# Row sums of the first norm taken from x's column tiles by ScalarE and GpSimd, and the first seven-product block in the order m1 m2 m7 m6 m4 m5 m3 with PSUM banks of its own for m3

## The chip, the cores and the metric

The kernel runs on one NeuronCore of a Trainium2 chip. Its time is device microseconds of one execution, and the median of several executions is compared. The engines are named as in the profile: PE (TensorE, matmul), PEld (its weight loads), DVE (VectorE), ACT (ScalarE), POOL (GpSimd) and SP (SyncE, which here only issues DMAs). DMAs are issued on the queues of SP, ACT and POOL. Each engine takes its own instructions in the order in which the program lists them; engines wait for each other through semaphores.

## The reference

One layer of an encoder on 512 tokens of width 2048, batch 1, in float32:

```python
def rmsnorm(x, g):
    xf = x.astype(jnp.float32)
    y = xf * lax.rsqrt(jnp.mean(xf * xf, axis=-1, keepdims=True) + EPS)
    return (y * g.astype(jnp.float32)).astype(x.dtype)

h = rmsnorm(x, g_mix)
proj = jnp.einsum('bsd,de->bse', h, w_in)          # (512, 2048) @ (2048, 4608)
qa, ka, va, qb, kb, vb = jnp.split(proj, offs, axis=-1)
...
x = x + jnp.einsum('bse,ed->bsd', mixed, w_out)
h2 = rmsnorm(x, g_ffn)
gate, up = jnp.split(jnp.einsum('bsd,df->bsf', h2, w_gate_up), 2, axis=-1)
x = x + jnp.einsum('bsf,fd->bsd', jax.nn.silu(gate) * up, w_down)
return rmsnorm(x, g_final)
```

Between them stand two attention mixers. Only the first norm and the first part of the input projection matter here. The norm's row factor r1 (one number for each of the 512 tokens) does not enter the projection's operands: the projection is computed from x times g_mix, and r1 is multiplied in when a result leaves PSUM. So r1 is needed only from the first eviction that uses it.

## The kernel before

**Numbers.** Every float32 operand of a matmul is split in two parts (`split`): the high part is an ACT copy to the type float32r, the low part a DVE subtraction of source and high part. A product is three matmuls (`mm3`, lines 230 to 232: high by high, high by low, low by high), each of 128x128 weights on 512 columns.

**Units.** The work of PE is a list of units in a fixed order. For each unit n the main loop at the end of the function first prepares (`x_prep` of tile n+1 while n is below 16; `prepare`, which issues weight loads and weight splits for units up to a set number of microseconds ahead by the plan's own clock), then multiplies, then runs the hooks that other code has registered for n with `hook(n, f)`. So the order on every engine's queue is written out by this loop. At most 8 pairs of split weights (`tw`) exist, so splits are at most 8 units ahead.

**The first chunk, units 0 to 15.** It multiplies x with the 512 columns of w_in that give kA and vA. x arrives as 16 column tiles `xs[k]` (512 tokens by 128 columns, as 128x512), loaded by SP. `x_prep(k)` transposes the tile on PE into a PSUM bank, copies it on ACT with the gain into `xpair` (line 326), makes the high part on ACT (line 327) and the low part on DVE (line 328). The unit then runs 12 matmuls. Two and three units after each pair of tiles, `x_sums` (four DVE operations of 256 columns, line 348) and `x_split` (two ACT copies, line 343, and two DVE subtractions, line 344) make the sums of x's quarters that the seven-product blocks need. Before that, POOL copies one of the parts that they overwrite to DRAM (`ar`, line 331); the split waits for this copy. After unit 15 ACT evicts four banks to tiles and sends them to DRAM (`kvA`, line 464).

**The column blocks, units 16 to 71 and 72 to 127.** Each multiplies x with 1024 columns of w_in by a seven-product scheme (Strassen's in Winograd's form): seven products m1 to m7 of half the size in each direction, each 8 units of 6 matmuls, 336 matmuls a block. For m7, m6, m5 and m4 DVE first adds or subtracts two weight tiles (line 792), then splits (ACT line 755, DVE line 758); for m1, m2 and m3 there is only the split. The products are summed up in three pairs of PSUM banks: m1, m6, m5 and m3 on pair z, m7 and m4 on pair y, m2 on pair x. A result is made in two steps: `begin` copies a pair of banks to an `ends` tile on ACT (line 840), `close` adds another pair to it on DVE (line 845) and POOL stores it; `only` is a `begin` with a store by ACT. Each multiplies r1 in. Where a product goes on summing on banks that are still to be read, its first matmul waits for that eviction. The first block's order is m1 m2 m7 m6 m5 m4 m3, and m1 is evicted seven units after its end, because r1 is late; the second block's order is m1 m7 m6 m2 m5 m4 m3.

**Row sums.** For r1 the kernel reads x a second time: eight loads of 128 tokens by 1024 columns on SP's queue (line 360, 512 KB each, two buffers), and eight squares on ACT with a row sum as side result (line 363), hooked to units 13 to 28. `make_r1` at unit 29 adds the halves on DVE and raises to the power -1/2 on POOL (line 212).

**Homes.** Tiles of x and of weights land in `homes`, a first-in first-out list of 20 tiles of 128x512 (`stage`). `x_prep` gives x's tile back as soon as its transposes are listed; a weight tile comes back after its last use. From unit 21 `more_homes` adds four tiles, and `fewer_homes` takes them out again in the second block. A load into a home waits for the last reader of what was there.

Of the kernel before, what the change touches and what calls it, by code (L numbers as in the profile page):

```python
# [11 lines left out]
F32 = mybir.dt.float32  # L12
# [7 lines left out]
P = 128  # L20
S = 512
D = 2048
# [34 lines left out]
HEAD_RATE = (1.42, 1.9)  # L57
TURN_LAG = 6
VALUE_LAG = 8
COLUMN_BLOCKS = 2  # L60


# [5 lines left out]
def encoder_block(ctx, tc, x, g_mix, w_in, g_q_a, g_k_a, g_out_a, g_out_b, w_out, g_ffn,  # L68
# [15 lines left out]
    def slot(base, dtype=F32, shape=(P, 512)):  # L84
        return sp.tile(list(shape), dtype, tag="s", name=nm(base))
# [14 lines left out]
    def release(*tiles):  # L100
        banks.extend(tiles)
# [12 lines left out]
    extra_homes, retired = [], []  # L114

    def more_homes():
        more = wp.tile([P, 4, 512], F32, tag="more", bufs=1, name="more")
        extra_homes.extend(more[:, n] for n in range(4))
        homes.extend(extra_homes)

    def fewer_homes():
        kept = [h for h in homes if not any(h is e for e in extra_homes)]
        homes.clear()
        homes.extend(kept)
        retired.extend(extra_homes)

    def leave_homes():
        homing[0] = False
# [32 lines left out]
    nc.scalar.activation(slot("table")[:, :1], ones, AF.Copy)  # L161
    warm_ps = bank()

    def warm_up(n):
# [143 lines left out]
    def x_prep(k):  # L308
        ps = bank()
        for t in range(NT):  # L310
            nc.tensor.transpose(ps[:, t * P:(t + 1) * P], xs[k][:, t, :], ident)
        homes.append(xs[k].rearrange("p t c -> p (t c)"))
        i, half = divmod(k, 2)
        if half == 0:
            xpair[i] = in_turn(pairs_turn, 3, [P, 4 * 512], F32, "xpair")
        flat = xpair[i][:, half * 1024:half * 1024 + 512]
        view = flat.rearrange("p (f c) -> p f c", c=256)
        hi, lo = (arena[half][:, 0:2, i, j] for j in range(2))
        gain = gm[:, k:k + 1]
        if k == 0:  # L320
            ps3 = ps.rearrange("p (f c) -> p f c", c=256)
            nc.scalar.activation(hi, ps3, AF.Copy, scale=gain)
            nc.vector.scalar_tensor_tensor(lo, ps3, gain, f32(hi), op0=OP.mult, op1=OP.subtract)
            nc.scalar.activation(flat, ps, AF.Copy, scale=gain)
        else:
            nc.scalar.activation(flat, ps, AF.Copy, scale=gain)
            nc.scalar.activation(hi, view, AF.Copy)
            nc.vector.tensor_tensor(lo, view, f32(hi), op=OP.subtract)
        release(ps)
        if half == 0:  # L330
            hook(k, lambda: nc.gpsimd.dma_start(ar_dram[:, i], arena[0][:, 1, i]))
        else:
            hook(k + 2, lambda: x_sums(i))
            hook(k + 3, lambda: x_split(i))
# [16 lines left out]
        tt(s2, s1, a_l)  # L351
        tt(s4, b_l, s2)

    ss1 = small(2 * NT)
    rows, rows_turn = {}, []

    def load_rows(n):
        rows[n] = in_turn(rows_turn, 2, [P, D // 2], F32, "rows")
        t, half = divmod(n, 2)
        nc.sync.dma_start(rows[n], x[0, t * P:(t + 1) * P, half * (D // 2):(half + 1) * (D // 2)])  # L360

    def row_squares(n):
        nc.scalar.activation(rows[n], rows[n], AF.Square, accum_out=ss1[:, n:n + 1])

    for n, at in enumerate((13, 15, 18, 20, 22, 24, 26, 28)):
        hook(at - 3, lambda n=n: load_rows(n))
        hook(at, lambda n=n: row_squares(n))

    def col_sums(src):
        ps = bank()  # L370
# [8 lines left out]

    def make_r1():  # L380
        ss = small()
        nc.vector.tensor_reduce(ss, ss1.rearrange("p (t c) -> p t c", c=2), axis=AX.X, op=OP.add)
        r1["r"] = rsqrt_mean(ss, NT, D)
        r1["rs"] = small()
        nc.vector.tensor_scalar(r1["rs"], r1["r"], HD ** -0.5, None, op0=OP.mult)

    tabs = {}

    hook(29, make_r1)
    hook(21, more_homes)  # L390

    def table_tasks():
        tasks = []
# [367 lines left out]
            self.box.multiply(self)  # L761

    class ColBlock:
        def __init__(self, w, row, lo, pairs, plan, tag, ready=None, close=None, chain=CHAIN):
            self.pairs, self.plan, self.ready, self.close = pairs, plan, ready, close
            self.ps, self.at, self.held = {}, {}, []

            def raw(i, j, q):
                at = row + (2 * q + i) * P
                return Raw(lambda t: [(w[0, at:at + P, lo[j]:lo[j] + 512], t)], tag=tag, width=512)  # L770
            kinds = {"a": (0, 0), "b": (0, 1), "c": (1, 1), "d": (1, 0), "e": (0, 1), "f": (1, 0), "g": (1, 1)}
            self.raws = [{n: raw(i, j, q) for n, (i, j) in kinds.items()} for q in range(pairs)]
            order = [(form, q) for form in chain for q in range(pairs)]
            if ready is not None:
                rest = order[6:8] + order[8:3 * pairs] + order[3 * pairs + 6:]
                order = order[:6] + order[3 * pairs:3 * pairs + 6] + rest
# [16 lines left out]
            return t[dst]  # L793

        def bank_of(self, form):
            name = CHAIN_BANK[form]
            if name not in self.ps:
                self.ps[name] = [bank() for _ in range(2)]
            return self.ps[name]

        def multiply(self, u):
            dst, i = self.bank_of(u.form), u.i
            if self.ready is not None:
                drain_until(lambda: self.ready[i])
            ending = self.close is not None and u.form == "m3"
            if ending:
                self.held.append(u)
            for t in range(1 if ending else 2):
                mm3(dst[t], cols(form_of(u.form, i), t * P), (u.pair[:, 0], u.pair[:, 1]),
                    u.form in ("m1", "m7", "m2") and i == 0, i == self.pairs - 1, True)  # L810
            if ending and i == self.pairs - 1:
                self.close(self)

        def done(self, form):
            release(*self.ps.pop(CHAIN_BANK[form]))

        def after(self, form, late, f):
            hook(self.at[form] + late, f)
# [3 lines left out]
    def in_block(names, lo):  # L822
        first = not blocks
        box = ColBlock(w_in, 0, lo, KD // 2, REREAD, "craw0" if first else "craw",
                       chain=("m1", "m2", "m7", "m6", "m5", "m4", "m3") if first else CHAIN)
        blocks.append(box)
        out = {}

        def rows_of(form, i, j, f, late=0):
            box.after(form, late, lambda: [f(form, j, 2 * i + t, t) for t in range(2)])  # L830
            if form in LAST_OF_BANK:
                box.after(form, late, lambda: box.done(form))

        def begin(form, j, row, t):
            if not ends:
                ends.extend(sp.tile([P, 2, 512], F32, tag="ends", bufs=3, name=nm("ends")) for _ in range(3))
            if t == 0:
                ends.append(ends.pop(0))
            out[j, row] = ends[-1][:, t]
            nc.scalar.activation(out[j, row], box.bank_of(form)[t], AF.Copy,  # L840
                                 scale=row_scale_of(names[j])[:, row:row + 1])

        def close(form, j, row, t):
            e = out[j, row]
            nc.vector.scalar_tensor_tensor(e, box.bank_of(form)[t], row_scale_of(names[j])[:, row:row + 1], e,
                                           op0=OP.mult, op1=OP.add)
# [12 lines left out]

    blocks, ends = [], []  # L860

# [16 lines left out]
    last.after("m5", 0, fewer_homes)  # L878
# [481 lines left out]
```

## Time and profile before

| | before |
|---|---|
| three runs | 2024.49 us median, 2023.68 to 2028.52 |
| span of the profiled execution | 2023.3 us |
| mean granted TensorE clock | 0.996 |
| first matmul of unit 0 / of the first block / of the second block / behind it | 7.14 / 57.95 / 143.35 / 219.51 us |
| DMA | 394.81 MB, mean 195 GB/s |

Of the profiled execution only the span, from its first to its last instruction, is given; the runs' times contain what lies around it. In the profile's rows, times are microseconds from the span's start and durations are microseconds unless marked ns. A row of the timeline reads: start, duration, engine, line of the code, operation, output<-input by the program's names, shapes, count; in brackets the idle time of that engine before it and what ended it. A grouped row reads: line, engine, operation, names and shapes, count | busy us, mean ns of one | idle us before them, and what ended it. A row of busy times by stretch reads: start:end and length, then for each engine its busy time and number of instructions, the granted clock, the share of the 16 DMA engines' time, and GB/s. Matmuls are pipelined: one of 128x512 shows 0.39 us, but in an unbroken row they start 0.227 us apart.

### The profile page before, as it was taken

The numbers are of one execution on the slowest core, as the hardware profiler recorded it, in microseconds if no ns is written. First come the engines' busy times: TensorE is split into PE (matmuls) and PEld (weight loads), VectorE is DVE, ScalarE is ACT, GpSimd is POOL, SyncE is SP. The second block draws the span as 40 slices with busy tenths as digits, with TensorE's granted clock in tenths as the row PEclk, the third lists the DMA queues.
The fourth block names the chain that finished last, engine by engine and source line by source line (L and its number), as shares of the span: only waits on it lengthen the run. The fifth ranks groups of instructions, "written<-read, shape, count | busy, mean of one in ns | idle before, by whom it ended". The sixth has DMA issues, their size and how long they took to land. (4 is left out here: it accounts for less than half of the span.)

```text
span 2023.3 us, 27380 instructions
## 1 busy us (share of the span) xinstructions
PE 1989.5 (98%) x9019; PEld 1632.9 (81%) x9019; DVE 1558.8 (77%) x2771; ACT 1112.5 (55%) x1964; POOL 125.9 (6%) x155
## 2 busy tenths in 40 slices
PE   9999999999999999999999999999999999999997
PEld 7778887887788888888888888888888887788886
DVE  6778866576754688878877878778789887977977
ACT  6655344455553565555555555545546665666656
POOL 0000100000010000000000000000000121111122
PEclk9999999999999999999999999999999999999999
DMA  9777533335343546647647558458467698768855
GB/s 293 239 251 235 185 115 103 99 111 171 98 151 133 184 167 203 239 136 266 220 163 273 186 184 285 153 192 296 133 227 267 189 248 260 196 168 270 198 128 190
DMA packets 232671, 394.81 MB, mean 195 GB/s; under 512 B 21536, under 2 KB 70480, under 8 KB 232400
## 3 DMA queue, kind: packets, MB, share of 16 engines
q1 hardware_dynamic: 206032, 330.33, 48.5%
q0 software_dynamic: 14800, 32.51, 7.9%
q10 hardware_dynamic: 11696, 30.23, 4.3%
q8 instruction: 70, 1.15, 0.2%
q14 instruction: 73, 0.60, 0.1%
HBM read 329.28 MB, written 63.70 MB: 194 GB/s over the span
## 5 line engine op out<-in xcount | busy, mean ns | idle before, releaser
L230 PE MATMUL b<-tw,arena 128*128 128x512 f32 x2136 | 838.5, 393 | 7.2 <-ACT ends L840 2.5
L231 PE MATMUL b<-tw,arena 128*128 128x512 f32 x2136 | 834.0, 390 | 5.4 <-DVE tw L758 5.1
L232 PE MATMUL b<-tw,arena 128*128 128x512 f32 x2136 | 832.8, 390 | 0.0
L755 ACT ACTIVATE tw<-raw 128x512 fp32r<-128x512 f32 x924 | 559.3, 628 | 441.2 <-DVE raw L792 286.6
L758 DVE TENSOR_TENSOR tw<-raw,tw 128x512 fp32r<-128x512 f32 x924 | 619.3, 687 | 173.1 <-ACT tw L755 170.1
L231 PEld LDWEIGHTS b<-tw,arena 128*128 128x128 f32 x2136 | 401.6, 188 | 93.3 <-DVE tw L758 12.3
L230 PEld LDWEIGHTS b<-tw,arena 128*128 128x128 f32 x2136 | 401.4, 188 | 90.7 <-ACT tw L755 3.3
L232 PEld LDWEIGHTS b<-tw,arena 128*128 128x128 f32 x2136 | 401.4, 188 | 83.9
L792 DVE TENSOR_TENSOR raw<-raw,raw 128x512 f32<-128x512 f32 x528 | 361.7, 685 | 0.8 <-DMA raw<-in_w_gate_up_dram 0.6
L230 PE MATMUL b<-w,arena 128*128 128x512 f32 x368 | 146.7, 399 | 0.0
L232 PE MATMUL b<-w,arena 128*128 128x512 f32 x368 | 144.3, 392 | 0.0
L231 PE MATMUL b<-w,arena 128*128 128x512 f32 x368 | 144.1, 392 | 0.0
L1127 POOL DMA_DIRECT2D x1d<-ev x76 | 66.4, 977 | 1157.5 <-ACT ev L1126 1156.5
L232 PEld LDWEIGHTS b<-w,arena 128*128 128x128 f32 x368 | 69.5, 189 | 15.1
L231 PEld LDWEIGHTS b<-w,arena 128*128 128x128 f32 x368 | 69.6, 189 | 13.9
L230 PEld LDWEIGHTS b<-w,arena 128*128 128x128 f32 x368 | 69.5, 189 | 13.7
L758 DVE TENSOR_TENSOR tw<-stage,tw 128x512 fp32r<-128x512 f32 x93 | 62.2, 687 | 23.5 <-ACT tw L755 23.4
L755 ACT ACTIVATE tw<-stage 128x512 fp32r<-128x512 f32 x93 | 56.5, 627 | 41.8 <-DVE stage L792 29.5
L222 DVE TENSOR_TENSOR pTl<-b,pTh 128x512 fp32r<-128x512 f32 x64 | 44.0, 688 | 36.1 <-ACT pTh L221 25.4
L287 DVE TENSOR_TENSOR w<-raw,w 128x512 fp32r<-128x512 f32 x96 | 64.7, 684 | 5.7 <-ACT ends L840 3.0
L348 DVE TENSOR_TENSOR pair<-pair 128x256 f32<-128x256 f32 x120 | 45.5, 421 | 27.3 <-ACT pair L983 21.9
L1126 ACT ACTIVATE ev<-b,smalls 128x512 f32<-128x512 f32 x76 | 49.7, 683 | 29.2 <-PE b L232 28.0
(186 smaller groups left out, 1749.2 us busy)
## 6 DMA issues: line engine op xcount, KB each, us to landing
raw<-in_w_gate_up_dram SPq DMA_DIRECT2D x616, 256.0 KB, 5.3
raw<-in_w_down_dram SPq DMA_DIRECT2D x176, 256.0 KB, 6.9
stage<-in_w_in_dram SPq DMA_DIRECT2D x114, 256.0 KB, 5.1
forms<-pair SPq DMA_DIRECT2D x22, 896.0 KB, 5.3
x1d<-ev POOLq DMA_DIRECT2D x76, 256.0 KB, 6.6
fr<-forms ACTq DMA_DIRECT2D x35, 512.0 KB, 5.5
raw<-in_w_in_dram SPq DMA_DIRECT2D x64, 256.0 KB, 4.2
raw<-in_w_out_dram SPq DMA_DIRECT2D x32, 512.0 KB, 4.8
```

The costliest lines, as they stand in the source:

```text
L222: nc.vector.tensor_tensor(lo, src, f32(hi), op=OP.subtract)
L230: nc.tensor.matmul(dst, ah, bh, start=start, stop=False, skip_group_check=chained)
L231: nc.tensor.matmul(dst, ah, bl, start=False, stop=False, skip_group_check=chained)
L232: nc.tensor.matmul(dst, al, bh, start=False, stop=stop, skip_group_check=chained)
L287: nc.vector.tensor_tensor(self.w[1], self.src, f32(self.w[0]), op=OP.subtract)
L348: nc.vector.tensor_tensor(out, x, y, op=op)
L755: nc.scalar.activation(self.pair[:, 0], self.src, AF.Copy)
L758: nc.vector.tensor_tensor(self.pair[:, 1], self.src, f32(self.pair[:, 0]), op=OP.subtract)
L792: nc.vector.tensor_tensor(t[dst], t[src[0]], t[src[1]], op=OP.add if form == "m6" else OP.subtract)
L1126: nc.scalar.activation(e, box.bank_of(form)[t], AF.Copy, scale=r2["r"][:, row:row + 1])
L1127: nc.gpsimd.dma_start(x1_dram[2 * cb + j, row], e, accum_op=OP.add)
```

## The change

**Row sums.** The second reading of x goes. `row_squares(k)` is now called at the end of `x_prep(k)`: ACT squares the tile `xs[k]` in place after its transposes, and POOL adds the squares of tiles 1 to 15 to that of tile 0 in an accumulator `sq1` of 128x512. `make_r1` moves from unit 29 to unit 20 and reduces `sq1` over 128 columns for each of the four token groups. The tile goes back to `homes` after the square and the add, no longer after the transposes. The space of the two row buffers becomes four tiles `early`: one is the accumulator, three are additional homes until unit 12 (a tile of x that lies in one of them by then comes back to the list later).

**The first block.** m4 comes before m5. m3 sums up alone on two banks of its own (pair x, after m2's have been released), instead of on z. So m5, the last on z, is read twice: by the `close` of result (1,1), and by a `begin` of result (0,1), to which a `close` after m3 adds m3's banks. m1 is evicted right at its end. The second block is left as it was.

**Small.** The first ACT instruction, which loads the table, writes to a column of `smalls` instead of to a tile of its own. On PE's queue the number and kind of instructions are the same.

```diff
-    def more_homes():
-        more = wp.tile([P, 4, 512], F32, tag="more", bufs=1, name="more")
...
+    def more_homes(name, tile):
+        extra_homes[name] = [tile[:, n] for n in range(4)]
+        homes.extend(extra_homes[name])
...
 (x_prep)
             nc.tensor.transpose(ps[:, t * P:(t + 1) * P], xs[k][:, t, :], ident)
-        homes.append(xs[k].rearrange("p t c -> p (t c)"))
...
         release(ps)
+        row_squares(k)
...
-    def load_rows(n):
-        rows[n] = in_turn(rows_turn, 2, [P, D // 2], F32, "rows")
-        t, half = divmod(n, 2)
-        nc.sync.dma_start(rows[n], x[0, t * P:(t + 1) * P, half * (D // 2):(half + 1) * (D // 2)])
-
-    def row_squares(n):
-        nc.scalar.activation(rows[n], rows[n], AF.Square, accum_out=ss1[:, n:n + 1])
-
-    for n, at in enumerate((13, 15, 18, 20, 22, 24, 26, 28)):
-        hook(at - 3, lambda n=n: load_rows(n))
-        hook(at, lambda n=n: row_squares(n))
+    early = sp.tile([P, 4, 512], F32, tag="rowss", bufs=1, name="early")
+    more_homes("early", early)
+    sq1 = [homes.pop()]
+
+    def row_squares(k):
+        home = xs[k].rearrange("p t c -> p (t c)")
+        if k == 0:
+            nc.scalar.activation(sq1[0], home, AF.Square)
+        else:
+            nc.scalar.activation(home, home, AF.Square)
+            nc.gpsimd.tensor_tensor(sq1[0], sq1[0], home, op=OP.add)
+        homes.append(home)
...
-        nc.vector.tensor_reduce(ss, ss1.rearrange("p (t c) -> p t c", c=2), axis=AX.X, op=OP.add)
+        nc.vector.tensor_reduce(ss, sq1[0].rearrange("p (t c) -> p t c", t=NT), axis=AX.X, op=OP.add)
...
-    hook(29, make_r1)
-    hook(21, more_homes)
+    hook(20, make_r1)
+    hook(21, lambda: more_homes("more", wp.tile([P, 4, 512], F32, tag="more", bufs=1, name="more")))
+    hook(EARLY_HOMES, lambda: fewer_homes("early"))
...
 (ColBlock.__init__)
+            self.banks = dict(CHAIN_BANK, m3="x") if apart else CHAIN_BANK
+            self.last_of_bank = LAST_OF_BANK + ("m5",) if apart else LAST_OF_BANK
+            self.opening = ("m1", "m7", "m2") + (("m3",) if apart else ())
...
 (in_block)
-                       chain=("m1", "m2", "m7", "m6", "m5", "m4", "m3") if first else CHAIN)
+                       chain=("m1", "m2", "m7", "m6", "m4", "m5", "m3") if first else CHAIN, apart=first)
...
-        rows_of("m1", 0, 0, begin, 7 if first else 0)
+        rows_of("m1", 0, 0, begin)
...
-        rows_of("m5", 1, 1, close)
+        rows_of("m5", 1, 1, close, not first)
         rows_of("m4", 1, 0, close)
-        rows_of("m3", 0, 1, only)
+        if first:
+            rows_of("m5", 0, 1, begin)
+            rows_of("m3", 0, 1, close)
+        else:
+            rows_of("m3", 0, 1, only)
```

More of the change, by code (lines that the diff above doesn't have):

```diff
@@ L59 @@
 VALUE_LAG = 8
+EARLY_HOMES = 12
 COLUMN_BLOCKS = 2
@@ L113, in encoder_block, with fewer_homes @@
     homing = [True]
-    extra_homes, retired = [], []
-    def more_homes():
-        more = wp.tile([P, 4, 512], F32, tag="more", bufs=1, name="more")
[L118 to L122, printed above, removed]
+    extra_homes, retired = {}, []
+    def more_homes(name, tile):
+        extra_homes[name] = [tile[:, n] for n in range(4)]
+        homes.extend(extra_homes[name])
+    def fewer_homes(name):
+        kept = [h for h in homes if not any(h is e for e in extra_homes[name])]
         homes.clear()
         homes.extend(kept)
-        retired.extend(extra_homes)
+        retired.extend(extra_homes[name])
     def leave_homes():
@@ L160, in encoder_block @@
     nc.vector.memset(warm, 0.0)
-    nc.scalar.activation(slot("table")[:, :1], ones, AF.Copy)
+    nc.scalar.activation(small(1), ones, AF.Copy)
     warm_ps = bank()
@@ L352, in form_sums @@
         tt(s4, b_l, s2)
-    ss1 = small(2 * NT)
-    rows, rows_turn = {}, []
-    def load_rows(n):
-        rows[n] = in_turn(rows_turn, 2, [P, D // 2], F32, "rows")
-        t, half = divmod(n, 2)
-        nc.sync.dma_start(rows[n], x[0, t * P:(t + 1) * P, half * (D // 2):(half + 1) * (D // 2)])
-    def row_squares(n):
-        nc.scalar.activation(rows[n], rows[n], AF.Square, accum_out=ss1[:, n:n + 1])
-    for n, at in enumerate((13, 15, 18, 20, 22, 24, 26, 28)):
-        hook(at - 3, lambda n=n: load_rows(n))
-        hook(at, lambda n=n: row_squares(n))
+    early = sp.tile([P, 4, 512], F32, tag="rowss", bufs=1, name="early")
[9 more added lines that the diff above has]
+        homes.append(home)
     def col_sums(src):
@@ L763, in encoder_block, with __init__ @@
     class ColBlock:
-        def __init__(self, w, row, lo, pairs, plan, tag, ready=None, close=None, chain=CHAIN):
+        def __init__(self, w, row, lo, pairs, plan, tag, ready=None, close=None, chain=CHAIN, apart=False):
             self.pairs, self.plan, self.ready, self.close = pairs, plan, ready, close
+            self.banks = dict(CHAIN_BANK, m3="x") if apart else CHAIN_BANK
+            self.last_of_bank = LAST_OF_BANK + ("m5",) if apart else LAST_OF_BANK
+            self.opening = ("m1", "m7", "m2") + (("m3",) if apart else ())
             self.ps, self.at, self.held = {}, {}, []
@@ L795, in bank_of @@
         def bank_of(self, form):
-            name = CHAIN_BANK[form]
+            name = self.banks[form]
             if name not in self.ps:
@@ L809, in multiply @@
                 mm3(dst[t], cols(form_of(u.form, i), t * P), (u.pair[:, 0], u.pair[:, 1]),
-                    u.form in ("m1", "m7", "m2") and i == 0, i == self.pairs - 1, True)
+                    u.form in self.opening and i == 0, i == self.pairs - 1, True)
             if ending and i == self.pairs - 1:
@@ L814, in done @@
         def done(self, form):
-            release(*self.ps.pop(CHAIN_BANK[form]))
+            release(*self.ps.pop(self.banks[form]))
         def after(self, form, late, f):
@@ L824, in in_block, with rows_of @@
         box = ColBlock(w_in, 0, lo, KD // 2, REREAD, "craw0" if first else "craw",
-                       chain=("m1", "m2", "m7", "m6", "m5", "m4", "m3") if first else CHAIN)
+                       chain=("m1", "m2", "m7", "m6", "m4", "m5", "m3") if first else CHAIN, apart=first)
         blocks.append(box)
         out = {}
[L829 to L832, printed above, removed]
+        def rows_of(form, i, j, f, ending=True):
+            box.after(form, 0, lambda: [f(form, j, 2 * i + t, t) for t in range(2)])
+            if form in box.last_of_bank and ending:
+                box.after(form, 0, lambda: box.done(form))
         def begin(form, j, row, t):
@@ L877, in encoder_block @@
     last.after("m3", 0, leave_homes)
-    last.after("m5", 0, fewer_homes)
+    last.after("m5", 0, lambda: fewer_homes("more"))
     last.after("m3", 1, lambda: reload("qA0", qA[0]))
```

## The prediction

> **What bounds the kernel now.** I read the page first, then the busy time of three stretches, then the waits of PE inside the one that the change touches.
>
> ```profile
> span 2023.3 us, 27380 instructions
> PE 1989.5 (98%) x9019; PEld 1632.9 (81%) x9019; DVE 1558.8 (77%) x2771; ACT 1112.5 (55%) x1964; POOL 125.9 (6%) x155
> ```
>
> PE is the bound over the whole span, so a change off PE pays only where PE stands still. From the timeline of PE, the first chunk's 16 units run from 7.14 to 57.95 us, the first column block from 57.95 to 143.35, the second from there to 219.52. The busy time of these stretches:
>
> ```profile
> core 0: us, PE busy (x) PEld busy (x) DVE busy (x) ACT busy (x) POOL busy (x), PEclk, DMA share, GB/s
> 7.14:57.95 50.81, 50.81 (x254) 41.87 (x253) 37.28 (x71) 38.59 (x68) 4.45 (x8) 1.00 0.91 288
> ...
> 57.95:143.35 85.40, 80.01 (x337) 63.50 (x336) 64.93 (x111) 48.88 (x85) 4.37 (x7) 0.98 0.74 261
> 143.35:219.52 76.17, 76.17 (x338) 63.07 (x337) 59.59 (x102) 38.29 (x64) 3.79 (x7) 1.00 0.70 230
> ```
>
> Both column blocks have 336 matmuls of 128x512. The second needs 76.17 us (0.227 each), the first 85.40. The difference, 9.23 us, is all that the first block can give back. The first chunk has no PE gap to give. Where the 9.23 go, from PE's timeline (the bracket is the idle time before and what ended it):
>
> ```profile
> 65.34 0.50 PE L231 MATMUL b<-tw,arena 128*128 128x512 f32 x1 [0.20 <-DVE tw L758]
> ...
> 82.87 0.49 PE L230 MATMUL b<-tw,arena 128*128 128x512 f32 x1 [1.35 <-ACT tw L755]
> ...
> 91.66 0.50 PE L231 MATMUL b<-tw,arena 128*128 128x512 f32 x1 [0.53 <-DVE tw L758]
> ...
> 110.58 0.50 PE L230 MATMUL b<-tw,arena 128*128 128x512 f32 x1 [2.53 <-ACT ends L840]
> ```
>
> Three places: late splits in m1 (64 to 70 us; the row shown is the first of three), a late split at the end of m2 with a slow stretch behind it (81 to 93; here lies the dip that leaves the block's granted clock at 0.98, about 1.7 us of 85.40), and the wait of m5's first matmul for m6's eviction. Counted from start to start against 0.227 they cost about 1.6, 4.7 and 2.8 us, 9.1 of the 9.23. ACT's timeline shows what was late:
>
> ```profile
> 81.15 1.06 ACT L363 ACTIVATE rows<-rows 128x1024 f32<-128x1024 f32 x1 [4.38 <-DMA rows<-in_x_dram]
> ...
> 82.21 1.13 ACT L755 ACTIVATE tw<-stage 128x512 fp32r<-128x512 f32 x2
> ...
> 109.86 1.25 ACT L840 ACTIVATE ends<-b,smalls 128x512 f32<-128x512 f32 x2
> ```
>
> ACT takes its queue in order. A row square waited 4.38 us for its rows, and the split that PE needed at 82.87 stood behind it.
>
> **What the change takes away.** The eight 512 KB row loads leave SP's queue and the eight squares (1.06 us each) leave ACT's between 51 and 85 us. That removes the wait behind the stall at 82.87; with it go the clock dip behind it and DVE's lateness at 91.66 (DVE idled for ACT and then had sum and split for every unit). I take back the whole 4.7. In m1, ACT loses three squares between 60 and 70 us but keeps the four kvA evictions; I take back 1.2 of 1.6. The order m4 before m5 gives m6's eviction eight units' time before its banks are written again, and m3 has banks of its own: 2.8 back. The two banks for m3 were not in use by then. Together 8.7.
>
> The moved m1 eviction (1.25 us of ACT) needs r1, now made at unit 20, three units before m1 ends. m5 gains two evictions on ACT, and m3 trades two on ACT for two on DVE:
>
> ```profile
> L845 DVE SCALAR_TENSOR_TENSOR ends<-b,smalls,ends 128x512 f32<-128x512 f32 x12 | 8.5, 750 | 8.2 <-PE b L232 8.2
> ```
>
> That is 1.5 us of DVE behind m3, where the second block's m1 begins with one split of 0.69 (L758) for 1.36 us of PE (six matmuls): nothing on the path, 1.5 if DVE had no room. SP, rid of the row loads, issues weights earlier; loads were not what PE waited for.
>
> **What it adds.** Sixteen squares 128x512 on ACT and fifteen adds 128x512 on POOL, all inside the first chunk. Their nearest rows:
>
> ```profile
> L603 POOL TENSOR_TENSOR acc<-acc,sq 128x512 f32<-128x512 f32 x14 | 18.1, 1292 | 259.0 <-ACT sq L602 221.7 <-DVE smalls L565 37.4
> ```
>
> *ACT.* A copy 128x512 from SBUF starts 0.52 us after the one ahead (9.05 below is two in 1.14). Sixteen make 8.5 us on 38.59 busy of 50.81: there is room, except at the start:
>
> ```profile
> 9.05 1.14 ACT L282 ACTIVATE tw<-stage 128x512 fp32r<-128x512 f32 x2
> 9.79 1.29 DVE L287 TENSOR_TENSOR tw<-stage,tw 128x512 fp32r<-128x512 f32 x2
> ...
> 10.66 0.39 PE L231 MATMUL b<-tw,arena 128*128 128x512 f32 x1
> ```
>
> The squares of tiles 0 and 1 stand ahead of the split at 9.05. It moves by 2 x 0.52, its DVE half from 9.79 to 10.8, that one ends near 11.5, and the matmul of 10.66 starts 0.85 later. I take 0.9.
>
> *POOL against DVE.* Here the sum is decided. A POOL add and a DVE instruction that began under it:
>
> ```profile
> 407.10 1.29 POOL L603 TENSOR_TENSOR acc<-acc,sq 128x512 f32<-128x512 f32 x1 [24.14 <-ACT sq L602]
> 407.52 1.15 DVE L570 TENSOR_SCALAR p<-p,smalls 128x512 f32<-128x512 f32 x1
> ```
>
> The whole group of that DVE line (least, median and most ns):
>
> ```profile
> L570 DVE TENSOR_SCALAR p<-p,smalls x64: 485/487/1151, 261.6 to 581.0; 128x512 f32<-128x512 f32 x64
> ```
>
> What usually takes 487 ns took 1151, and ended 0.28 us after the add. The other way round, POOL's pow of 128x4 with DVE idle, behind a DVE tensor-tensor of 256 columns, and behind one of 512:
>
> ```profile
> 85.43 1.04 POOL L212 TENSOR_TENSOR smalls<-smalls,fixed 128x4 f32<-128x4 f32 x1 [32.94 <-DVE smalls L210]
> ...
> 302.39 0.75 DVE L431 TENSOR_TENSOR ra<-qA,gsq 128x256 f32<-128x256 f32 x2
> 302.56 1.11 POOL L212 TENSOR_TENSOR smalls<-smalls,fixed 128x4 f32<-128x4 f32 x1 [7.39 <-DVE smalls L210]
> ...
> 744.26 0.69 DVE L792 TENSOR_TENSOR raw<-raw,raw 128x512 f32<-128x512 f32 x1
> 744.43 1.39 POOL L212 TENSOR_TENSOR smalls<-smalls,fixed 128x4 f32<-128x4 f32 x1 [144.69 <-DVE smalls L210]
> ```
>
> The longer the tensor-tensor in front, the longer the pow: it waits for it. No row has a DVE tensor-tensor that begins under a 128x512 add, so what an add costs DVE lies between 0 and 1.29 us. I take the upper end, because each of the two rows shows one engine shut out while the other runs, and because all but one of DVE's instructions in the chunk are tensor-tensors with both inputs in SBUF, as at 744.26.
>
> [...]
>
> The room: DVE was busy 37.28 of 50.81 us in the chunk, idle 13.53, nearly all of it ahead of one group:
>
> ```profile
> L328 DVE TENSOR_TENSOR arena<-xpair,arena 128x512 fp32r<-128x512 f32 x15 | 10.4, 693 | 13.3 <-ACT arena L327 13.3
> ```
>
> L328 writes the low half of x for the next unit, so when DVE has no room PE waits. One of them, and the first matmul of its unit:
>
> ```profile
> 18.40 0.69 DVE L328 TENSOR_TENSOR arena<-xpair,arena 128x512 fp32r<-128x512 f32 x1 [1.90 <-ACT arena L327]
> 19.94 0.48 PE L230 MATMUL b<-tw,arena 128*128 128x512 f32 x1
> ```
>
> Fifteen adds take 15 x 1.292 = 19.4 us: 5.9 more than the idle time. The split ends at 19.09 for a matmul at 19.94, 0.85 ahead, and some of the chunk's last sums and splits, say 0.55, can slip past 57.95, where DVE still has gaps: 5.9 less 1.4 is 4.5. The bounds are 0 and, if each add costs a further 0.2 in handing over, 5.9 + 3.0 = 8.9.
>
> x tiles now come free behind square and add, later for the SP loads that take their place; four more homes until unit 12 stand against that, and the plan loads 24 us ahead: nothing, up to one add's 1.29 if SP ran dry. POOL's copies of x to DRAM queue behind two adds each, 2.6 us:
>
> ```profile
> ar<-arena POOLq DMA_DIRECT2D x8, 256.0 KB, 5.6
> ```
>
> Their reader, the split of x, comes four units or 12.7 us after the issue: 8.2 fit in. Two new waits for POOL stand on other queues: the kvA evictions go to homes that the last adds have read, and behind them on ACT stand the splits of m1; r1's reduction needs the last add, and behind it on DVE stand the splits of units 24 on. The last add is due near 54 us, the evictions from 56.5, the reduction from 64: nothing while POOL is less than two adds late, and about 1.3 for each add beyond, which only rival 2 brings.
>
> **The sum.** 2023.3 - 8.7 + 0.9 + 4.5 = 2020.0 of span. The three runs' median is 2024.49, 1.2 above the profiled span; with these, 2021.2.
>
> **The rivals.**
> 1. *The adds cost DVE nothing*: a tensor-tensor runs beside the add. For it: no row denies it for this pair. Against: the pow's 1.39. 2023.3 - 8.7 + 0.9 + 1.2 = 2016.7. Chance 0.24.
> 2. *DVE becomes the bound of the chunk, and the time ends above before's*: each add keeps DVE out for itself and for one tensor-tensor more, since L328 of the next unit queues behind the splits that the add held up. 37.28 + 15 x (1.29 + 0.69) = 67.0, 16.2 above 50.81; less 1.4 it is 14.8: 2023.3 - 8.7 + 0.9 + 14.8 + 1.2 = 2031.5. It decides from 1.52 us of DVE an add on, where the chunk loses the 7.8 that the block wins (13.53 + 1.4 + 7.8 over 15). Against: the row of 1151 ends 0.28 after the add, with no second wait. Chance 0.14.
> 3. *The rows were not the cause*: weights come late at 81 us all the same, and only the eviction's wait and m1's part go. 2023.3 - 4.0 + 0.9 + 4.5 + 1.2 = 2025.9. For it: 0.91 of the DMA engines' time was taken in the chunk. Against: ACT's row names the row load. Chance 0.10.
>
> **How the numbers follow.** A measurement of this kernel can tell about 0.3%, 6.1 us, from no change: faster is below 2018.4, slower above 2030.6. The forecast has 0.52, its own range 2017.7 to 2025.6 (adds from 1 to 8.9). Faster: nearly all of rival 1 (0.22) and a fifth of the forecast (0.11), 0.33. Slower: most of rival 2 (0.10) and a little of rival 3, 0.11. Within: 0.56. The range goes from below rival 1, 2015.5, to 2028, and leaves out rival 2's centre.
>
> **What would show it.** The first block takes 76 to 77 us, with no L840-like wait at m5 and no granted clock under 0.9. In the first chunk PE waits for DVE's split of x or tw, DVE tensor-tensors that start under an add last over 1 us, and the chunk takes 55 to 56 us. If those last 0.69 throughout, rival 1 holds; if the chunk takes over 62, rival 2; if PE still waits near 81 us with DMA as the releaser, rival 3. The forecast is wrong if the second block or anything behind it changes by over 1 us.

## The result, and the profile after

| | before | changed |
|---|---|---|
| median of 11 runs each | 2026.12 us (2023.68 to 2030.17) | 2021.18 us (2019.47 to 2024.38) |
| ratio, 95% interval | | 0.998, 0.9972 to 0.9988 |
| profiled execution, span (its time) | 2023.3 (2024.49) | 2022.6 (2024.38, the longest of its eleven) |

The median lies at the predicted 2021.2, and the change, 4.9 us or 0.24%, is within the 0.3% that the prediction called no change (the eleven runs of before lie 0.32% apart). The three runs of before that the prediction had are among the eleven; with all of them the median is 1.6 higher. So the agreement of the total is luck: the working, a saving of 3.3 us, set on the median of all eleven gives 2022.8, and by stages the changed kernel is only 1.46 us ahead at 219 us (below); the rest of its 4.9 us seems to lie in code that the change does not touch. The stages tell more.

The lengths below are read from PE's timeline, from the first matmul of a stage to that of the next, as in the prediction. "Unit 0" and "unit 1" are the first two units of the chunk; an undisturbed one takes 3.2. The experiments are explained below.

| us | first matmul | unit 0 | unit 1 | first chunk | first block | second block | its end | span |
|---|---|---|---|---|---|---|---|---|
| before | 7.14 | 3.21 | 3.19 | 50.81 | 85.40 | 76.16 | 219.51 | 2023.3 |
| changed | 7.49 | 3.94 | 4.25 | 57.31 | 77.09 | 76.16 | 218.05 | 2022.6 |
| e1_no_adds | 6.30 | 4.33 | 3.71 | 52.45 | 77.89 | 76.16 | 212.80 | 2014.5 |
| e2_adds_on_dve | 7.23 | 3.89 | 3.79 | 52.09 | 77.83 | 76.16 | 213.31 | 2016.1 |
| e3_order_only | 7.42 | 3.86 | 3.19 | 51.46 | 82.77 | 76.16 | 217.81 | 2018.9 |
| e4_sums_only | 6.99 | 3.78 | 4.37 | 57.32 | 77.41 | 76.16 | 217.88 | 2019.1 |
| e5_late_squares | 7.08 | 4.31 | 3.22 | 51.93 | 77.85 | 76.16 | 213.02 | 2015.8 |
| e6_adds_twice | 7.11 | 4.25 | 3.93 | 72.34 | 76.95 | 76.16 | 232.56 | 2033.9 |
| e7_two_loads | 7.09 | 4.42 | 3.21 | 52.04 | 79.06 | 76.16 | 214.35 | 2013.8 |
| e8_best | 7.09 | 3.88 | 3.19 | 51.48 | 77.24 | 76.16 | 211.97 | 2012.3 |

The block gives back 85.40 - 77.09 = 8.31 us, and the chunk takes 57.31 - 50.81 = 6.50 more. With a start 0.35 later, the second block ends 1.46 earlier.

The changed kernel's page, and its busy time in the same three stretches:

```profile
span 2022.6 us, 27400 instructions
...
PE 1989.3 (98%) x9019; PEld 1633.7 (81%) x9019; DVE 1572.3 (78%) x2773; ACT 1113.3 (55%) x1964; POOL 149.9 (7%) x172
```

```profile
7.49:64.80 57.31, 53.19 (x252) 41.95 (x251) 49.48 (x70) 46.23 (x82) 27.22 (x23) 1.00 0.75 231
64.80:141.89 77.09, 76.75 (x338) 62.91 (x336) 65.71 (x112) 43.33 (x73) 4.36 (x7) 1.00 0.74 255
141.89:218.05 76.16, 76.16 (x338) 63.06 (x336) 60.82 (x105) 36.23 (x60) 4.91 (x9) 1.00 0.70 232
```

PE's work over the span is the same (1989.5 before). In the block 0.34 us of its idle time is left (before: 5.39) and the granted clock is 1.00. In the chunk, PE, which had no idle time, now has 57.31 - 53.19 = 4.12; DVE's busy time rose from 37.28 to 49.48, POOL's from 4.45 to 27.22. Where PE waits, from its timeline:

```profile
12.67 0.50 PE L232 MATMUL b<-tw,arena 128*128 128x512 f32 x1 [0.77 <-DVE tw L288]
...
29.66 0.50 PE L233 MATMUL b<-tw,arena 128*128 128x512 f32 x1 [0.46 <-DVE arena L328]
...
62.40 0.50 PE L233 MATMUL b<-tw,arena 128*128 128x512 f32 x1 [1.07 <-DVE arena L328]
...
78.06 0.50 PE L232 MATMUL b<-tw,arena 128*128 128x512 f32 x1 [0.34 <-DVE tw L758]
```

The first is unit 1's. The next two are the first and the last of five waits for the low half of x, in units 6, 9, 11, 13 and 15. None of the waits that the prediction showed in the block is left; the one of 0.34 is new, and stands early in m2, 2.1 us behind its first matmul (e8 below has its cause). What made DVE late is seen in POOL's and DVE's timelines of the same stretch:

```profile
24.38 1.79 POOL L365 TENSOR_TENSOR early<-early,stage 128x512 f32<-128x512 f32 x1 [1.38 <-issue]
...
52.90 1.29 POOL L365 TENSOR_TENSOR early<-early,stage 128x512 f32<-128x512 f32 x1 [1.54 <-issue]
```

```profile
24.33 0.68 DVE L328 TENSOR_TENSOR arena<-xpair,arena 128x512 fp32r<-128x512 f32 x1
24.93 1.78 DVE L288 TENSOR_TENSOR tw<-stage,tw 128x512 fp32r<-128x512 f32 x1
...
59.10 2.65 DVE L349 TENSOR_TENSOR xpair<-xpair 128x256 f32<-128x256 f32 x4
...
65.28 1.54 DVE L349 TENSOR_TENSOR xpair<-xpair 128x256 f32<-128x256 f32 x4
```

The add of 24.38 came while DVE's L328 was running (24.33 to 25.01): it lasts 1.79 where an undisturbed one takes 1.29. The split L288 that was started at 24.93 then lasts 1.78, where L328 takes 0.68 for the same shape: it ends at 26.71, 0.54 after the add (24.38 + 1.79 = 26.17). So each engine waits for the other's instruction; a split that falls under an add comes 1.1 later. Four sums of x under an add take 2.65, without one 1.54, again 1.1.

### The profile page after: what moved, and what is told of

It is laid out like the page before. It is cut to its first block, busy times and chain, and to the rows that moved or that the text cites. A ratio compares the mean times of both kernels' runs of the same rounds, so it can differ in the third digit from the quotient of the medians.

```text
span 2022.6 us, 27400 instructions
## 1 busy us (share of the span) xinstructions
PE 1989.3 (98%) x9019; PEld 1633.7 (81%) x9019; DVE 1572.3 (78%) x2773; ACT 1113.3 (55%) x1964; POOL 149.9 (7%) x172
## 5 line engine op out<-in xcount | busy, mean ns | idle before, releaser
L288 DVE TENSOR_TENSOR w<-raw,w 128x512 fp32r<-128x512 f32 x96 | 64.7, 684 | 5.6 <-ACT w L283 3.2
L1037 DVE TENSOR_TENSOR s<-b,s 128x512 f32<-128x512 f32 x66 | 44.0, 687 | 24.8 <-PE b L233 24.8
```

The lines of the kernel that those rows point to most:

```text
L288: nc.vector.tensor_tensor(self.w[1], self.src, f32(self.w[0]), op=OP.subtract)
L1037: nc.vector.tensor_tensor(d[:, t], box.bank_of(form)[t], d[:, t], op=OP.add)
```

## The experiments

Two theories stood against each other. *T*, that of the prediction: the adds on POOL cost the chunk about 4.5 us through DVE, and the row loads and the order give the block 8.7. *R*, its rivals: the adds cost nothing or far more, or the row loads were not the cause. Ratios are against runs of before on the same chip: median 2025.68 (16 runs) for the first four, 2025.23 (9 runs) for the last four.

**e1_no_adds**, against the changed kernel:

```diff
-            nc.gpsimd.tensor_tensor(sq1[0], sq1[0], home, op=OP.add)
```

> The changed kernel without its fifteen GpSimd adds (r1 is then made from the squares of tile 0 alone). If it is the adds that hold up DVE (theory): DVE's tensor-tensors of 512 columns in the first chunk all last 0.69 us, none 1.7 to 1.8; the five waits of PE for line 328 in the chunk are gone and the chunk takes 51.5 to 52.5 us instead of 57.3; the first block stays at 76.5 to 77.5; span 5 to 6 us shorter, near 2016 to 2017.5. If it is the sixteen squares on ACT or the homes that come free late (rival): the chunk stays above 55 us, with PE waiting for ACT or DMA.

Measured: chunk 52.45, span 2014.5, 2016.24 us in one run. The five waits for L328 are gone, no DVE instruction of 512 columns in the chunk takes over 0.75 us, and the chunk is 57.31 - 52.45 = 4.86 shorter. The block, 77.89, is somewhat above the expected 76.5 to 77.5. Its stretch:

```profile
6.30:58.75 52.45, 51.63 (x252) 41.84 (x251) 38.29 (x71) 44.83 (x81) 4.45 (x8) 1.00 0.84 263
```

ACT still does its squares (44.83 busy against 38.59 in before). What is left over before's 50.81 is 1.64, and units 0 and 1 hold all of it (1.12 and 0.52): behind them the squares cost nothing.

**e2_adds_on_dve**, the same adds on DVE itself:

```diff
-            nc.gpsimd.tensor_tensor(sq1[0], sq1[0], home, op=OP.add)
+            nc.vector.tensor_tensor(sq1[0], sq1[0], home, op=OP.add)
```

> The fifteen adds on DVE instead of GpSimd. Theory: an add keeps DVE busy for 0.60 us, less than the 1.1 us for which a GpSimd add shuts it out; 37.3 + 9 = 46.3 us fit into the chunk, so the chunk takes 51.5 to 53 us, and the time is 3 to 5 us under that of the changed kernel, 0.995 to 0.997 of the kernel before. Rival (DVE's room in the chunk is what counts, whoever adds; or the adds' wait for ACT's squares stops DVE's queue): the chunk stays at 55 us or more.

Measured: chunk 52.09, median 2017.47 (4 runs), ratio 0.9956 (0.9941 to 0.9971). The chunk is 5.22 shorter than with the adds on POOL.

```profile
7.23:59.32 52.09, 51.77 (x253) 42.39 (x251) 45.22 (x85) 44.84 (x81) 4.45 (x8) 1.00 0.81 255
```

With fifteen more instructions of its own DVE is busy for 45.22 us; with the adds on POOL it was 49.48. Doing an add (0.68 us on DVE) costs DVE less than being shut out by one: over before's 37.28 its busy time rose by 7.94 in all, against 12.20 with the adds on POOL. Over before's 50.81 the chunk has 1.28, and units 0 and 1 hold it all (0.68 and 0.60): the adds on DVE cost nothing.

**e3_order_only**, against before; the row loads and squares stay:

```diff
-                       chain=("m1", "m2", "m7", "m6", "m5", "m4", "m3") if first else CHAIN)
+                       chain=("m1", "m2", "m7", "m6", "m4", "m5", "m3") if first else CHAIN, apart=first)
...
-        rows_of("m5", 1, 1, close)
+        rows_of("m5", 1, 1, close, 0, not first)
```

(with the new banks of m3 and the two results of m5 and m3 as in the change; m1 is still evicted seven units late)

> The kernel before with the new order and banks of the first block alone; row loads and row squares as before, m1 still evicted seven units late. Theory: the wait at the start of m5 (2.8 us) goes and nothing else; first chunk 50.8, first block 82.6 us, time 2 to 3 us under before (0.9985 to 0.999). Rival (the eviction wait only moves to another place in the block, or later splits become the bound): block over 84 us.

Measured: block 82.77, median 2020.66 (9 runs), ratio 0.9977 (0.9967 to 0.9987). By product, from PE's timeline, the first four take 12.56, 12.56, 14.13 and 10.88, where before has 12.52, 12.40, 14.13 and 13.58. So the order alone takes away m5's wait, 2.7, and nothing else. The time is 5.0 us under before's, more than the expected 2 to 3; the last section comes back to this.

**e4_sums_only**, against the changed kernel: the new row sums with the old order and banks.

```diff
-                       chain=("m1", "m2", "m7", "m6", "m4", "m5", "m3") if first else CHAIN, apart=first)
+                       chain=("m1", "m2", "m7", "m6", "m5", "m4", "m3") if first else CHAIN)
...
-        if first:
-            rows_of("m5", 0, 1, begin)
-            rows_of("m3", 0, 1, close)
-        else:
-            rows_of("m3", 0, 1, only)
+        rows_of("m3", 0, 1, only)
```

> The changed kernel with the first block in the old order and banks. Theory: the chunk takes 57 us as in the changed kernel, the block keeps one wait at m5 of 2 to 3 us and takes 79 to 80; time 2 to 3 us above the changed kernel, 0.998 to 1.001 of before: the row sums alone give about as much in the block as they take in the chunk. Rival (the stalls of m1 and m2 came from something else than the row loads and squares): the block stays above 82 us.

Measured: block 77.41, median 2020.85 (8 runs), ratio 0.9976 (0.9965 to 0.9987). The block is shorter than the expected 79 to 80, and the ratio lower than the expected 0.998 to 1.001. This was not foreseen: with m5 on the same banks as in before its wait falls to 0.26 (m6 11.14 against 10.88). m6's eviction on ACT, in this kernel:

```profile
106.79 0.63 ACT L755 ACTIVATE tw<-stage 128x512 fp32r<-128x512 f32 x1 [0.57 <-DVE stage L795]
108.21 1.37 ACT L843 ACTIVATE ends<-b,smalls 128x512 f32<-128x512 f32 x2 [0.79 <-PE b L233]
```

and the split ahead of it in before, whose eviction began at 109.86 in the prediction's row:

```profile
106.91 0.63 ACT L755 ACTIVATE tw<-stage 128x512 fp32r<-128x512 f32 x1 [0.57 <-DVE stage L792]
108.12 0.63 ACT L755 ACTIVATE tw<-stage 128x512 fp32r<-128x512 f32 x1 [0.57 <-PE b L232]
109.32 0.63 ACT L755 ACTIVATE tw<-stage 128x512 fp32r<-128x512 f32 x1 [0.57 <-DVE stage L792]
```

Here ACT has its splits behind it, and waits 0.79 for PE. In before it still had two splits to do when m6's matmuls ended (110.58 less the wait of 2.53 is 108.05), and all stand at the pace of DVE, which has a sum and a split (0.6 each) for every unit: they come 1.2 apart. A unit of PE takes 1.36, so DVE and ACT catch up only 0.16 a unit, and at 110 us they had not made up for the stall of 82. So m5's wait was for the most part a late part of the row loads' cost (e7 below: 1.7 of its 2.8), which the order removes too. The two parts of the change do not add up: the order is worth 2.63 alone, and 77.41 - 77.09 = 0.32 beside the new sums.

**e5_late_squares**, e2 with the squares of tiles 0 and 1 listed behind unit 0's splits:

```diff
-        row_squares(k)
+        if k < 2:
+            hook(0, lambda: row_squares(k))
+        else:
+            row_squares(k)
```

> Adds on DVE, and the squares of tiles 0 and 1 listed after the first weight splits instead of ahead of them. Theory (the two squares hold up the split that unit 1 needs): unit 1 takes 3.2 us instead of 3.8, the chunk 51 to 51.6, the block 77.5 to 78. Rival (unit 1 is late because of the first loads): unit 1 stays at 3.7 to 4.2.

Measured: unit 1 takes 3.22 (3.79 in e2), the chunk 51.93, one run 2017.56. So the two squares (with tile 1's add behind them) cost unit 1 0.57. The chunk is 0.3 above the expected 51 to 51.6: what is left over 50.81 lies in unit 0 alone, 4.31 against 3.21. Unit 0 differs from one execution to another whatever the squares do: 3.86 in e3 and 4.42 in e7, neither of which has a square near it, and 3.88 in e8, whose chunk is the same code as here. PE's first matmuls show why, first in the changed kernel, then in before:

```profile
8.06 0.63 PE L232 MATMUL b<-tw,arena 128*128 128x512 f32 x1
8.49 0.63 PE L233 MATMUL b<-tw,arena 128*128 128x512 f32 x1
8.91 0.49 PE L231 MATMUL b<-tw,arena 128*128 128x512 f32 x1
```

```profile
7.45 0.39 PE L231 MATMUL b<-tw,arena 128*128 128x512 f32 x1
7.68 0.40 PE L232 MATMUL b<-tw,arena 128*128 128x512 f32 x1
7.91 0.40 PE L230 MATMUL b<-tw,arena 128*128 128x512 f32 x1
```

They start 0.43 apart, and 0.23 in before: PE is still at half pace. In the traces' clock records the clock rises to full at 6.4 us in before, at 9.1 in the changed kernel, 8.5 in e8, 9.5 in e5 and 9.8 in e7. (In e1 and e4 it rises before unit 0; there unit 0 ends in a wait of 0.51 and 0.34 for an ACT split.)

**e6_adds_twice**, every add of the changed kernel done twice:

```diff
             nc.gpsimd.tensor_tensor(sq1[0], sq1[0], home, op=OP.add)
+            nc.gpsimd.tensor_tensor(sq1[0], sq1[0], home, op=OP.add)
```

> The changed kernel with every GpSimd add done twice in a row (the row sums then count tiles 1 to 15 twice). Theory: each add shuts DVE out for about 1.1 us whenever DVE has tensor-tensors to do; 37.3 + 30 x 1.1 = 70.3 us of DVE time in the chunk, so the chunk takes 66 to 73 us instead of 57.3. Rival (DVE and the adds mostly share, and the loss comes from how x's tiles or squares are ordered): the chunk stays below 61.

Measured: chunk 72.34, one run 2035.64. PE waits four times for 2.3 to 3.0 us, each time for L328. The first of these waits, then the busy time of the chunk, of the 4 us behind that wait, and of the 7 us that follow:

```profile
28.89 0.50 PE L233 MATMUL b<-tw,arena 128*128 128x512 f32 x1 [3.01 <-DVE arena L328]
```

```profile
7.11:79.45 72.34, 61.07 (x253) 47.58 (x251) 68.77 (x71) 45.96 (x82) 50.24 (x38) 0.88 0.62 191
```

```profile
28.80:33.00 4.20, 4.11 (x13) 3.19 (x14) 4.20 (x7) 2.40 (x5) 2.07 (x2) 0.62 0.62 192
33.00:40.00 7.00, 7.00 (x36) 5.68 (x35) 6.96 (x8) 5.79 (x12) 5.42 (x5) 0.98 0.25 77
```

Now DVE is full, 68.77 of 72.34. The clock falls behind each of these waits (granted 0.62 from 28.80 to 33.00, and 0.58, 0.60 and 0.50 in the 4 us behind the other three), but DVE has no idle time in the first of these stretches (4.20 of 4.20), so it is DVE that sets the pace there too. Fifteen more adds cost the chunk 15.0 us, 1.0 each, where the first fifteen cost 5: the bound changes from PE with waits to DVE, the outcome of the prediction's rival 2, only at twice the adds.

**e7_two_loads**, against before: two of the eight row loads, all eight squares on what these brought.

```diff
-        nc.scalar.activation(rows[n], rows[n], AF.Square, accum_out=ss1[:, n:n + 1])
+        nc.scalar.activation(rows[n % 2], rows[n % 2], AF.Square, accum_out=ss1[:, n:n + 1])
...
-        hook(at - 3, lambda n=n: load_rows(n))
+        if n < 2:
+            hook(at - 3, lambda n=n: load_rows(n))
```

> The kernel before with only two of the eight row loads; all eight squares run, on these two buffers (the row sums are then wrong). Theory (ACT's squares wait for row loads that land late, and behind them the splits): the stall at the end of m2 and the clock dip behind it go, ACT's squares wait for no DMA, and with DVE no longer behind, the wait at the start of m5 goes as well, as it did with the row sums changed alone; m1 keeps 1 us or more of its lateness because the squares stay on ACT. First block 77.5 to 80 us instead of 85.4. Rival (the squares' time on ACT is the cause, not their loads): the block stays above 82.

Measured: block 79.06, one run 2015.56, the only edit being that six loads are not made. The squares on ACT, in this kernel:

```profile
L363 ACT ACTIVATE rows<-rows x8: 1042/1046/1061, 52.4 to 78.7; 128x1024 f32<-128x1024 f32 x8
...
  ACT stage L465: 0.4, 1
```

and in before:

```profile
L363 ACT ACTIVATE rows<-rows x8: 1042/1052/1062, 51.2 to 83.8; 128x1024 f32<-128x1024 f32 x8
...
  DMA rows<-in_x_dram: 6.7, 3
```

The lines below each give ACT's idle time ahead of the squares and its cause: 6.7 us for the row loads in before, none here. The squares, as many and as long, stay. PE's waits in the block are then

```profile
PE b L230 <- ACT ends L841: 0.9, 1, 0.9
PE b L231 <- DVE tw L759: 0.7, 2, 0.4
```

The stall at the end of m2 and the slow stretch behind it are gone (m2 10.91, m7 10.88), m5's wait is 0.9 instead of 2.5, and m1 stays at 12.60. So the six loads cost 85.40 - 79.06 = 6.34 of the block's 9.23. What remains with the squares on ACT is 1.7 in m1 and 1.2 around m5's wait.

**e8_best**, e5 with one small DVE operation of `make_r1` moved:

```diff
+        hook(30, make_rs)
+
+    def make_rs():
         r1["rs"] = small()
         nc.vector.tensor_scalar(r1["rs"], r1["r"], HD ** -0.5, None, op0=OP.mult)
```

In the changed kernel this operation waits on DVE for POOL's power, with six splits behind it:

```profile
77.24 0.17 DVE L384 TENSOR_SCALAR smalls<-smalls 128x4 f32<-128x4 f32 x1 [1.17 <-POOL smalls L213]
77.32 3.70 DVE L758 TENSOR_TENSOR tw<-stage,tw 128x512 fp32r<-128x512 f32 x6
```

> Adds on DVE, the first two squares late, and the factor rs (r1 times a constant, used only by later projections) computed on DVE at unit 30 instead of right behind GpSimd's power. Theory (DVE stands 1.17 us for the power and the splits of m2 come late): m2 takes 10.9 to 11.1 us instead of 11.5, the block 76.2 to 77.3, the chunk 51 to 51.6; time 0.994 to 0.996 of the kernel before. Rival: m2 stays at 11.5.

Measured: block 77.24 with m2 at 10.89 (11.50 in e2), chunk 51.48, median 2014.59 (2013.45 to 2018.32, 5 runs), ratio 0.9951 (0.9937 to 0.9964). It beats before and the changed kernel: the second block ends at 211.97, 7.54 before before's.

```profile
7.09:58.57 51.48, 51.48 (x252) 42.34 (x251) 45.31 (x85) 44.82 (x81) 4.46 (x8) 1.00 0.83 259
58.57:135.81 77.24, 76.77 (x337) 62.91 (x336) 65.65 (x113) 43.91 (x74) 4.75 (x7) 1.00 0.73 254
```

PE has no idle time in the chunk, and 0.47 in the block.

## Why the prediction was right, and where it was not

- **The block's 8.7.** Measured 8.31. By place: m1 1.36 (1.2 forecast; with the adds off POOL it is only 0.6, as e1 and e2 have m1 at 11.98 and 11.93, while e6 with its longer waits has 11.04, so part of it is time that the chunk's waits gave the splits), end of m2 and the stretch behind 0.89 + 3.25 = 4.14 (4.7), m5's wait with the little behind it 2.83 (2.8). The 4.7 of the old stall are gone whole; the 0.6 missing is a new loss in m2, the wait for the power (moved in e8, which has m2 at 10.89), a step that the prediction did not price: it named r1's reduction as a wait for the last add, not what DVE does while POOL raises to the power.
- **Its causes.** "2.8 back" for the order was right in size and incomplete in cause: the new row sums alone take it to 0.26 (e4). The prediction read the row that released PE and stopped there; the eviction's own lateness came from splits that were late, for the most part because of the row loads. That the loads, not the squares, caused the stall at 82 is shown by e7. Taking six loads out also leaves more of the DMA to the weights (0.71 of the DMA engines' time is taken in e7's block, 0.74 in before's), but these were not late in before: the two splits at 82.21 in the prediction's row follow the square without idle time. So rival 3 falls.
- **The clock dip** was listed among the costs of that stretch. The granted clock is 0.83 from 81.47 to 91.66 in before. In e3 the same stall came without a dip:

```profile
82.10:94.96 12.86, 9.09 (x37) 6.33 (x35) 9.55 (x18) 7.75 (x14) 2.20 (x3) 1.00 0.73 239
```

  Granted clock 1.00, yet m2 and m7 together take 26.69 us against 26.53 in before. PE simply waits longer for DVE (1.35 at 89.06 and 0.69 at 92.79) instead of running slowly: the dip lay over work that was late anyway, and cost nothing.
- **The start, 0.9.** Unit 1 lost 1.06; without the POOL adds 0.52 (e1) and 0.60 (e2). So the place was right, but the squares alone are about half of it, and the rest goes with the adds on POOL. The 0.73 of unit 0 and the 0.35 of the start were not forecast; unit 0 has PE's half pace up to 9.1 us in it (e5 above), which e3 and e7 have without any square.
- **The adds, 4.5.** Measured 57.31 - 50.81 less units 0 and 1 (0.73 and 1.06) = 4.71; by removal 4.86 (e1) and 5.22 (e2). The mechanism was right (a split of 0.68 lasts 1.78 under an add), the size came out right by luck: both sides of its working were off, and against each other. The price was too high: 1.29 an add forecast, the author's estimate between 0 and 1.29, which no row of before shows; measured are 1.1 for a split caught under one, and over the chunk DVE's busy time rose 49.48 - 37.28 = 12.2, or 0.81 an add, since some adds fall on idle time. The 0.2 of handing over in the prediction's upper bound no run shows: the split of 24.93 ends 0.54 behind the add, sooner than its own 0.68. And the cover was taken as perfect, 13.53 us all usable, which it is not:

```profile
L328 DVE TENSOR_TENSOR arena<-xpair,arena 128x512 fp32r<-128x512 f32 x15 | 11.3, 755 | 7.3 <-ACT arena L327 7.3
```

  DVE still idled 7.3 us ahead of L328 in the changed kernel while PE lost 4.7 to it elsewhere. With a rise of 12.2 and a cover of 13.53 the prediction's own sum would have come to nothing. The loss falls in single units, where one add catches the sums and the next a split (57.40 to 59.17 and 60.22 to 61.75 in unit 15), and idle time in another unit does not pay it back. Only with the adds doubled is DVE full, and then an add costs 1.0.
- **Its signs.** With unit 0, unit 1 and the adds together the chunk is 57.31, above the 55 to 56 that the prediction named, and the block's 77.09 is just above 76 to 77.
- **Rival 1** (adds free) falls by e1, **rival 2** by the chunk's 57.3.
- **"The second block or anything behind it" unchanged.** The second block takes 76.16 in all kernels. Behind it the profiled execution of the changed kernel is 0.8 longer than before's, but its median is 4.9 lower with only 1.46 of it visible at the second block's end (the changed kernel's profiled execution is its longest, before's the second shortest of its eleven). The next section says what is known of the rest.

## What to carry to other kernels

An idle engine is not free if its instructions hold up those of the engine that is nearly late: here a split under an add lasted 1.78 instead of 0.68, and the fifteen adds cost 5 us on POOL and nothing on DVE, though DVE was much the busier of the two. Cover is counted where it lies, unit by unit: 13.5 us idle in sum did not hide 12 us of delay. And before two waits are credited to two edits, ask why the second one's releaser was late; if it goes back to the first, only one of them pays.

## What was not expected of the hardware

**Code that the edits do not touch differs by several us.** From the end of the second block to the end of the span the profiled executions take 1803.8 (before), 1804.6 (changed) and 1799.5 to 1802.8 (the eight others). One place is near 333 us, where PE waits for a DVE split in every kernel. Before, the wait and the clock behind it:

```profile
333.22 0.50 PE L230 MATMUL b<-arena,qTh 128*128 128x512 f32 x1 [1.91 <-DVE pTl L222]
```

```profile
333.22:337.40 4.18, 4.18 (x12) 3.29 (x13) 2.99 (x6) 1.93 (x5) 0.00 (x0) 0.60 0.00 0
```

The changed kernel at the same place:

```profile
331.50 0.50 PE L231 MATMUL b<-arena,qTh 128*128 128x512 f32 x1 [1.59 <-DVE pTl L223]
```

```profile
331.50:335.50 4.00, 4.00 (x20) 3.34 (x21) 2.99 (x6) 1.79 (x4) 0.00 (x0) 1.00 0.00 0
```

Behind the longer wait PE runs at a granted clock of 0.60 for 4 us, behind the shorter one at full speed; with the wait itself that is about 2 us. The eight others wait 0.99 to 1.41 there, without a dip. In the changed kernel's profiled execution this was lost again near 1700 us, to a wait of 2.1 with a dip behind it. Medians fall by 2 to 3.5 us more than the first 220 us explain: e2 by 8.2 with 6.2 at the end of the second block, e3 by 5.0 with 1.7, e8 by 10.6 with 7.5, the changed kernel by 4.9 with 1.5. So before seems to be longer behind the second block in most of its executions. The granted clock fits that: its mean over the runs is 0.9964 (before, 16 runs) against 0.9973 (e3) and 0.9978 (e4), and 0.9960 (before, 9 runs) against 0.9976 (e8). A dip as at 333 (3.41 us at 0.50 in the clock record) costs about 0.0008 of the span of 2023.3, so before has one or two more of them in an execution, as an estimate (one can be that of 85 us, which cost nothing). Where they lie in the runs without a trace, and what makes the wait at 333 longer in before, was not tried, and stays open.

**A dip does not follow from a wait's length alone.** The clock fell behind waits of 1.35 us (82.87 in before), 1.91 and 2.3 to 3.0 (e6), and did not behind 1.51 (e3), 1.59 (changed) and 2.53 (m5's in before). Every kernel has one of 2.42 near 490 us: the clock fell there in nine of the ten, and not in e8. Two of these waits, and the clock around them:

```profile
108.05:112.20 4.15, 1.62 (x7) 1.36 (x8) 4.11 (x7) 3.42 (x6) 0.00 (x0) 1.00 0.92 305
```

```profile
482.30:488.00 5.70, 3.27 (x18) 2.76 (x18) 4.34 (x10) 3.19 (x7) 0.00 (x0) 1.00 0.56 214
```

The first is before's 2.53, the second e8's 2.42. What differs is where a wait falls. In the traces' clock records a dip is to 0.50 and lasts 3.41 us, or twice that (behind e6's last wait the granted clock is 0.50 from 71.40 to 75.60 and 0.74 from there to 79.45), and the dips of one execution begin whole steps of 3.41 apart: in before at 84.9, 334.1 and 494.5, which is 73 and 47 steps, in the changed kernel at 490.4, 1698.7 and 2005.9, which is 354 and 90. Counted by these steps, between 8 us and 12 us before the end of the ten executions, PE was idle for 1.8 us or more in fifteen of them, and a dip followed in the next step each time; of fourteen with 1.58 to 1.79 us it followed in seven; with less idle time no dip began. In before the steps ahead of its three dips have 1.58, 1.91 and 2.42, in the changed kernel 2.01, 2.12 and 1.69; no dip stands behind 1.79 (before), 1.66 and 1.54 (changed). The 2.53 of before lay across two steps, with 1.79 in the fuller one, and 1.77 of e8's 2.42 fell in one. So these traces show the border near half a step of idle time, 1.7 us (matmul ends are modelled, so it is not sharp).
